# A norm's broadcast, the normalizing of its tiles and the pooled branch, reordered in a two-block transformer kernel

## The chip, the cores and the metric

The kernel runs on one core of one Trainium2 chip. The metric is the device time of one execution in microseconds (us); lower is better. The engines are named as in the profile: PE does the matmuls and the transposes, DVE, ACT and POOL do elementwise work, SP starts the weight loads. Each engine has a queue of its own, and semaphores tie the queues together.

## What is computed

Two stacks of two layers each work on 256 tokens of width 1024; the first stack carries 256 context tokens beside them. Only the first stack's modulated norm, its mixer and the pooled branch in it matter here:

```python
def rms_norm(x, g):
    y = x * lax.rsqrt(jnp.mean(x * x, axis=-1, keepdims=True) + RMS_EPS)
    return y * g

def mod_norm(x, m, i, g):
    return rms_norm(x, g) * (1 + m[:, 3 * i + 1, None]) + m[:, 3 * i, None]

# first stack, layer l: ffn 0, then the mixer, then ffn 1
x = ffn_sublayer(x, m, 0, norm_g[l, 0], ffn_w_in[l, 0], ffn_w_out[l, 0])
h = mod_norm(x, m, 1, norm_g[l, 1])
u = h @ w_in[l]
y = jnp.concatenate([
    gated_conv_mixer(u[..., :OFF_B], u[..., OFF_B:OFF_C], u[..., OFF_C:OFF_P], conv_w[l]),
    multiscale_pool_mixer(u[..., OFF_P:OFF_Q], pool_w[l], pool_scale[l]),   # window mean - itself, @ pool_w
    neighbourhood_attention(q, k, v, kc, vc, rpb[l]),
], axis=-1) @ w_out[l]
x = x + m[:, 5, None] * y
x = ffn_sublayer(x, m, 2, norm_g[l, 2], ffn_w_in[l, 1], ffn_w_out[l, 1])
```

The context goes through the same mixer in layer 0, so that 512 columns are worked on there; in layer 1 its keys and values alone are needed, and the pooled branch has 256 columns. The second stack (`hybrid_layer`) has plain norms, three attentions, and a feed-forward part with a short convolution.

## The kernel before

**Layout.** Activations lie transposed: eight K tiles `X[kt]` of 128 channels by 512 (or 256) tokens. Each large product is made in three matmuls (`mm3`, L129 at `mm`): both operands are split into a rounded high part and the rest (`hi`, `lo`), and hi·hi, hi·lo and lo·hi are added up in PSUM. Weights are split as well (`begin`, L102 on ACT gives `whi`, L103 on DVE gives `wlo`), one chunk ahead of their use.

**Norm.** `modnorm` gives two kinds of operands. `pre` is the tile scaled but not yet normalized (`xhi`, `xlo`); the first projections run on it, and their results are multiplied by the norm's factor afterwards. `ops` are the normalized tiles (`hhi`, `hlo`) that all later projections take, made by `normed()` once the factor is there. `stats` begins the factor: squares, sums over channels on PE (`ms`, L176, into `pt`), the factor `r` (DVE L181, then a power on POOL, L182), and then `over`: four transposes on PE (L189, two for 256 tokens) that spread `r` over the partitions and a copy on DVE into `rb` (L191). A list of steps with ticks sets where in the code these two stand: `tick()` is called at half and at the end of each group of products; both steps have tick 0.

**Normalizing before.** For each K tile: `n = x * rb` on DVE (L238, 512 wide); scale and shift for each half of 256 (ACT L244, or DVE L242 for the second half of odd tiles); `hhi` as ACT's copy of `n` (L102); `hlo = n - hhi` on DVE (L103).

**Mixer (`mix1`).** The w_in chunks are used in the order 4 to 9 (queries, keys, values), 3 (pooled input `u`), then attention for four pairs of heads (scores `sc` L580, softmax on DVE and ACT, transposes `pt` L601, output `o` L678), then chunks 2, 0, 1 (the convolution), then w_out. ACT copies chunk 3's result into `z` (L658); POOL makes the window means from it (`pool_sums`, L730 to L743, then L649 and L650) into `su0` and `su1`. POOL also loads and turns a bias tile `tb` (L565, L566) for each head. At the end of the mixer `su` goes through one matmul each (L715), and w_out takes its eight K tiles in the order 0 to 7: 0 and 1 are the convolution, 2 and 3 the pooled branch, 4 to 7 the attention (`mhi`, `mlo`).

**Order.** The framework's scheduler takes the code as a list and sets the order in which each engine's instructions stand in its queue, by estimates of its own; an instruction can be put ahead of others that were written earlier if it finds room. On the chip each queue runs in the order in which it was laid down. Names below: mix(0), mix(1) are the mixers of layers 0 and 1, ffn(l,s) the feed-forward parts; "filler" are products of a later chunk that the scheduler put between steps of attention.

Of the kernel before, what the change touches and what calls it, by code (L numbers as in the profile page):

```python
# [8 lines left out]
F32 = mybir.dt.float32  # L9
BF16 = mybir.dt.bfloat16  # L10
F32R = mybir.dt.float32r
# [23 lines left out]
class Slots:  # L35
    """Tiles in slots of their own, handed out in the order in which the trace gives them back."""
# [19 lines left out]
class Kernel:  # L56
# [48 lines left out]
    def weights(self, *key):  # L105
        """The split of the next chunk in the order of use; the one after it is begun as well."""
        assert self.order[self.used] == key, (key, self.order[self.used])
        while len(self.ready) < 2 and self.begun < len(self.order):
            self.ready.append(self.begin(*self.order[self.begun]))
            self.begun += 1  # L110
        self.used += 1
        return self.ready.pop(0)
# [14 lines left out]
    def mm(self, *a, **k):  # L127
        """A product; while the chain is on, one after the other as they are written."""
        i = self.nc.tensor.matmul(*a, **k)  # L129
        if self.chain:  # L130
            if self.chained is not None:
                self.after(i, self.chained)
            self.chained = i
# [11 lines left out]
    def project(self, w, width, cols, ops, n):  # L145
        banks = [self.bank("mm") for _ in cols]
        k = len(ops)
        for i in range(k):
            for ps, c in zip(banks, cols):
                self.mm3(ps[:, :n], self.w_at(w, i, width, c), ops[i], i == 0, i == k - 1)  # L150
            if i in (k // 2 - 1, k - 1):
                self.tick()
        return banks
# [40 lines left out]
    def stats(self, X, n, at=(0, 0)):  # L194
        """Begins a norm's statistics; they are finished between the products of the next projections."""
        acc = self.squares(X, n)

        def ms():
            ps = self.bank("pt")
            self.sums(ps, acc, n)  # L200
            self.r = self.rsqrt(ps, n // 128)

        def over():
            self.rb = self.spread(self.r, n // 128)

        self.later(at, ms, over)

    def later(self, at, *steps):
        """Has the steps taken between the products that follow, by their halves."""
        self.steps, self.ticks = list(zip(at, steps)), -1  # L210
        self.tick()
# [6 lines left out]
    def modnorm(self, l, i, n, nd):  # L218
# [13 lines left out]
        self.stats(self.X, n, (0, 0))  # L232
        ops = []

        def normed():
            for kt in range(KT):
                t = self.act(name="n")
                nc.vector.tensor_tensor(t[:, :n], self.X[kt][:, :n], self.rb[:, :n], op=ALU.mult)  # L238
                for r in segs:
                    c = slice(r * 256, r * 256 + 256)  # L240
                    if r and kt % 2:
                        nc.vector.tensor_scalar(t[:, c], t[:, c], self.mod(l, i + 1, kt, r), self.mod(l, i, kt, r), op0=ALU.mult, op1=ALU.add)  # L242
                    else:
                        nc.scalar.activation(t[:, c], t[:, c], AF.Identity, bias=self.mod(l, i, kt, r), scale=self.mod(l, i + 1, kt, r))  # L244
                hi, lo = self.act(F32R, "hhi"), self.act(F32R, "hlo")
                self.split(hi[:, :n], lo[:, :n], t[:, :n])
                self.slots.free(t)
                ops.append((hi, lo))
# [3 lines left out]
    def first_gates(self, finish):  # L252
        """The first norm and two chunks of its gates, begun on the scales alone: the shifts are loaded last."""
# [287 lines left out]
    def preload(self, name):  # L541
        """Has ACT's next table set loaded behind the last function of the one before it."""
# [26 lines left out]
    def attn1(self, q, k, tbs):  # L569
        """The transposed weights of a pair of heads, whose scores take the two halves of the rows."""  # L570
# [34 lines left out]
    def mix1(self, l, fill=()):  # L605
# [80 lines left out]
        self.preload("silu_and_others")  # L686
        C = []
# [24 lines left out]
        for m in range(2):  # L712
            su = SU[m]
            pw = self.bank("mm")
            nc.tensor.matmul(pw[:, :n1], self.poolw[:, l, m, :], su[:, :n1], start=True, stop=True)  # L715
            sc = self.par["pool_scale"][:, l * 2 + m:l * 2 + m + 1]
            mix[2 + m] = hi, lo = pair()
            nc.scalar.activation(hi[:, :n1], pw[:, :n1], AF.Copy, scale=sc)
            nc.vector.scalar_tensor_tensor(out=lo[:, :n1], in0=pw[:, :n1], scalar=sc, in1=hi[:, :n1].bitcast(F32), op0=ALU.mult, op1=ALU.subtract)
        self.slots.free(*SU)  # L720

        for c in range(4):
            w = self.weights("w_out", l, c)
            for m2, ps in enumerate(self.project(w, 256, (0, 128), [(a[:, :n1], b[:, :n1]) for a, b in mix], n1)):
                self.residual(2 * c + m2, ps, l, 5, n1)
# [20 lines left out]
    def pair2(self, one, first, second):  # L746
        """The transposed weights of a pair of heads, whose scores take the two halves of the rows."""
# [83 lines left out]
    def edge(self):  # L831
# [17 lines left out]
        def ms():  # L849
            # r * (r * r * scaled + EPS) ** -0.5 with r = (plain + EPS) ** -0.5  # L850
# [22 lines left out]
    def layer2(self, L):  # L873
# [133 lines left out]
        self.stats(X, 256, (0, 0))  # L1007
# [231 lines left out]
```

## Time and profile before

| | us |
|---|---|
| median of three runs (lowest to highest) | 2641.17 (2639.41 to 2641.89) |
| span of the profiled execution | 2640.9 |
| PE busy | 2588.1 |
| DVE, ACT, POOL busy | 1754.1, 1175.7, 121.6 |

The stages, by the times at which they begin in the trace: ffn(0,0) 0, mix(0) about 409, ffn(0,1) 627, ffn(1,0) 995, mix(1) 1367, ffn(1,1) 1517, the second stack 1709 to the end. The page gives busy time for each engine, the clock granted to PE in tenths of full speed, and the chain of work that ended last. A timeline row is: start, duration, engine, line, operation, tiles, shapes, count; in brackets the idle time of the engine just before it and the instruction that ended it. A row with x4 is four instructions in a row, and its duration is that of all four.

### The profile page before, as it was taken

How to read it: one execution, taken by the hardware profiler on the slowest of the kernel's cores; microseconds unless marked ns; L12 is line 12 of the kernel's file. 1: busy time of each engine (PE TensorE's matmuls, PEld its weight loads, DVE VectorE, ACT ScalarE, POOL GpSimd, SP SyncE). 2: the span in 40 equal slices, each digit the busy share in tenths (PEclk: the TensorE clock that was granted, in tenths of full speed). 3: DMA queues.
4: the chain of work that ended last, by engine and by line, in shares of the span. 5: the costliest groups of instructions: out<-in, count | busy, mean ns of one | idle time of the engine just before them, and what ended most of it. 6: DMA issues, size and time to landing. Idle time of an engine off the chain costs nothing.

```text
span 2640.9 us, 40212 instructions
## 1 busy us (share of the span) xinstructions
PE 2588.1 (98%) x16220; PEld 2251.3 (85%) x16220; DVE 1754.1 (66%) x3259; ACT 1175.7 (45%) x2125; POOL 121.6 (5%) x196
## 2 busy tenths in 40 slices
PE   7999999999999999999999999999999999999999
PEld 5888888668888888888887899987999998799998
DVE  6877755557867758765354665666589866557984
ACT  4322234445222234212344554456556655654664
POOL 1000002200000000000002000002000000200000
PEclk9999999999999999999999999999999999999999
DMA  7545533112545533453233254632454463245444
GB/s 270 207 167 191 181 121 123 54 51 107 189 170 179 177 119 141 176 179 141 72 130 108 96 189 174 207 115 94 161 191 176 166 204 126 96 160 182 173 169 148
DMA packets 61114, 401.70 MB, mean 152 GB/s; under 512 B 7040, under 2 KB 7168, under 8 KB 21632
## 3 DMA queue, kind: packets, MB, share of 16 engines
q1 hardware_dynamic: 59616, 395.20, 42.3%
q0 software_dynamic: 1024, 3.15, 0.4%
q8 instruction: 127, 2.08, 0.3%
q10 hardware_dynamic: 288, 0.79, 0.1%
q14 instruction: 59, 0.48, 0.1%
HBM read 398.06 MB, written 1.05 MB: 151 GB/s over the span
## 4 chain that ended last, share of the span: by engine, by line
PE 85%; issue 8%; DVE 2%; ACT 2%; POOL 1%; DMA 0%; SPq 0%; POOLq 0%; DVEq 0%; ACTq 0%
PE mm L129 78%; PE sc L580 1%; PE sc L752 1%; PE o L804 1%; PE o L678 1%; PE pt L601 1%; DVE wlo L103 1%; PE pt L770 1%; ACT whi L102 1%; POOL ptw L797 1%; POOL nl L787 0%; POOL r L182 0%; PE o L806 0%; DMA raw<-in_w_mod 0%; PE sc L129 0%
## 5 line engine op out<-in xcount | busy, mean ns | idle before, releaser
L102 ACT ACTIVATE whi<-raw 128x1024 fp32r<-128x1024 f32 (+2 forms) x704 | 621.0, 925 | 544.9 <-PE mm L129 272.3
L103 DVE TENSOR_TENSOR wlo<-raw,whi 128x1024 fp32r<-128x1024 f32 (+2 forms) x704 | 730.0, 1065 | 172.4 <-ACT whi L102 171.2
L129 PE MATMUL mm<-hlo,whi 128*128 128x512 f32 (+1 forms) x1520 | 555.7, 366 | 2.9 <-DVE hlo L103 2.9
L129 PE MATMUL mm<-hhi,wlo 128*128 128x512 f32 (+1 forms) x1520 | 555.8, 366 | 0.0
L129 PE MATMUL mm<-hhi,whi 128*128 128x512 f32 (+1 forms) x1520 | 554.4, 366 | 0.0
L129 PEld LDWEIGHTS mm<-hlo,whi 128*128 128x128 f32 x1520 | 286.1, 188 | 54.8 <-DVE hlo L103 3.5
L129 PEld LDWEIGHTS mm<-hhi,wlo 128*128 128x128 f32 x1520 | 285.9, 188 | 52.2 <-issue 2.2
L129 PEld LDWEIGHTS mm<-hhi,whi 128*128 128x128 f32 x1520 | 285.7, 188 | 52.0 <-issue 1.9
L129 PE MATMUL mm<-xg,whi 128*128 128x256 f32 x1600 | 298.3, 286 | 0.0
L485 ACT ACTIVATE t<-mm 128x512 f32<-128x512 f32 (+1 forms) x82 | 44.7, 546 | 520.4 <-PE mm L129 520.4
L129 PEld LDWEIGHTS mm<-xg,whi 128*128 128x128 f32 x1600 | 249.3, 190 | 7.5 <-issue 6.4
L129 PE MATMUL mm<-h,whi 128*128 128x256 f32 x1280 | 227.7, 281 | 0.3
L129 PE MATMUL mm<-xg,wlo 128*128 128x256 f32 x800 | 227.8, 285 | 0.0
L129 PE MATMUL mm<-glo,whi 128*128 128x512 f32 x528 | 208.6, 395 | 0.0
L129 PE MATMUL mm<-ghi,whi 128*128 128x512 f32 x528 | 208.3, 395 | 0.0
L129 PE MATMUL mm<-ghi,wlo 128*128 128x512 f32 x528 | 207.7, 393 | 0.0
L129 PEld LDWEIGHTS mm<-h,whi 128*128 128x128 f32 x1280 | 196.3, 188 | 1.1 <-DVE h L103 1.1
L410 DVE CUSTOM_DVE_ANT_0 junk<-raw,cb,par 128x1024 bf16<-128x1024 f32 x128 | 163.9, 1280 | 49.3 <-DMA raw<-in_w_mod 48.4
L392 DVE SCALAR_TENSOR_TENSOR x<-mm,m,x 128x256 f32<-128x256 f32 x128 | 56.0, 479 | 192.3 <-PE mm L129 191.5
L129 PE MATMUL mm<-h,wlo 128*128 128x256 f32 x640 | 179.1, 281 | 0.0
L410 DVE CUSTOM_DVE_ANT_0 raw<-raw,cb,par 128x1024 f32<-128x1024 f32 x128 | 164.3, 1284 | 3.7
L129 PEld LDWEIGHTS mm<-xg,wlo 128*128 128x128 f32 x800 | 152.4, 190 | 4.1 <-issue 3.6
(270 smaller groups left out, 4099.4 us busy)
## 6 DMA issues: line engine op xcount, KB each, us to landing
raw<-in_ffn_w_in SPq DMA_DIRECT2D x87, 1024.0 KB, 4.8
raw<-in_w_in SPq DMA_DIRECT2D x74, 1024.0 KB, 4.8
raw<-in_w_mod SPq DMA_DIRECT2D x72, 1024.0 KB, 4.8
raw<-in_ffn_w_out SPq DMA_DIRECT2D x64, 704.0 KB, 4.0
raw<-in_w_up SPq DMA_DIRECT2D x44, 1024.0 KB, 4.8
raw<-in_w_down SPq DMA_DIRECT2D x32, 704.0 KB, 4.2
raw<-in_w_out SPq DMA_DIRECT2D x16, 1024.0 KB, 4.8
raw<-in_w_branch SPq DMA_DIRECT2D x12, 1024.0 KB, 4.8
```

What stands on the lines that cost most here:

```text
L102: self.nc.scalar.activation(hi, src, AF.Copy)
L103: self.nc.vector.tensor_sub(lo, src, hi.bitcast(F32))
L129: i = self.nc.tensor.matmul(*a, **k)
L392: self.nc.vector.scalar_tensor_tensor(out=self.X[m][:, c], in0=ps[:, c], scalar=self.mod(l, i, m, r), in1=self.X[m][:, c], op0=ALU.mult, o ...
L410: nc.vector.tensor_tensor_reduce(out=w if r else self.junk, in0=w, in1=self.cb[:, r, :], scale=1.0, scalar=self.par["b_mod"][:, c:c + 1], ...
L485: self.tabled(nc.scalar.activation(g[:, :n], pa[:, :n], AF.Silu))
L580: nc.tensor.matmul(sc[:, :nk], q[r, c0 + qt * 128:c0 + qt * 128 + 128], k[r, c0:c0 + nk], start=True, stop=True)
L601: nc.tensor.transpose(pp[:, kt * 128:kt * 128 + 128], s[:, kt * 128:kt * 128 + 128], self.ident)
L678: nc.tensor.matmul(o[64 * a:64 * a + 64, :256], v[:, h * 64:h * 64 + 64], pts[a][:, kt, :], start=(kt == 0), stop=(kt == len(vs) - 1), til ...
L752: self.nc.tensor.matmul(sc[:, o:o + n], a[r, ca:ca + 128], b[r, cb:cb + n], start=True, stop=True)
L770: nc.tensor.transpose(pp[:, (qt + i) * 128 if qt == 0 or i == 0 else 256:((qt + i) * 128 if qt == 0 or i == 0 else 256) + 128], s[:, a + i ...
L797: nc.gpsimd.tensor_tensor(pt[:, c:c + 128], pt[:, c:c + 128], self.past, op=ALU.mult)
```

## The change

Three edits.

1. `stats` still takes the sums at tick 0; the broadcast step `over` is put at tick 2, and at tick 3 for mix(0) (`i == 3 and n == nd`). A group of pre-products has 24 matmuls and one tick at its end. The second stack's feed-forward norm goes from (0, 0) to (0, 2) as well.
2. `normed()` works on halves of 256 in three steps: DVE makes `n = x * scale * rb`, ACT writes `hhi = n + shift` rounded, DVE makes `hlo = (n + shift) - hhi`.
3. The pooled branch's matmul, `mhi` and `mlo` are written right behind attention, ahead of w_in chunk 2, and w_out takes its K tiles in the order 4, 5, 6, 7, 2, 3, 0, 1.

```diff
-        self.stats(self.X, n, (0, 0))
+        self.stats(self.X, n, (0, 3 if i == 3 and n == nd else 2))
...
             for kt in range(KT):
                 t = self.act(name="n")
-                nc.vector.tensor_tensor(t[:, :n], self.X[kt][:, :n], self.rb[:, :n], op=ALU.mult)
+                hi, lo = self.act(F32R, "hhi"), self.act(F32R, "hlo")
                 for r in segs:
                     c = slice(r * 256, r * 256 + 256)
-                    if r and kt % 2:
-                        nc.vector.tensor_scalar(t[:, c], t[:, c], self.mod(l, i + 1, kt, r), self.mod(l, i, kt, r), op0=ALU.mult, op1=ALU.add)
-                    else:
-                        nc.scalar.activation(t[:, c], t[:, c], AF.Identity, bias=self.mod(l, i, kt, r), scale=self.mod(l, i + 1, kt, r))
-                hi, lo = self.act(F32R, "hhi"), self.act(F32R, "hlo")
-                self.split(hi[:, :n], lo[:, :n], t[:, :n])
+                    sh = self.mod(l, i, kt, r)
+                    nc.vector.scalar_tensor_tensor(out=t[:, c], in0=self.X[kt][:, c], scalar=self.mod(l, i + 1, kt, r), in1=self.rb[:, c], op0=ALU.mult, op1=ALU.mult)
+                    nc.scalar.activation(hi[:, c], t[:, c], AF.Identity, bias=sh)
+                    nc.vector.scalar_tensor_tensor(out=lo[:, c], in0=t[:, c], scalar=sh, in1=hi[:, c].bitcast(F32), op0=ALU.add, op1=ALU.subtract)
...
         self.preload("silu_and_others")
+        for m in range(2):
+            su = SU[m]
+            pw = self.bank("mm")
+            nc.tensor.matmul(pw[:, :n1], self.poolw[:, l, m, :], su[:, :n1], start=True, stop=True)
+            sc = self.par["pool_scale"][:, l * 2 + m:l * 2 + m + 1]
+            mix[2 + m] = hi, lo = pair()
+            nc.scalar.activation(hi[:, :n1], pw[:, :n1], AF.Copy, scale=sc)
+            nc.vector.scalar_tensor_tensor(out=lo[:, :n1], in0=pw[:, :n1], scalar=sc, in1=hi[:, :n1].bitcast(F32), op0=ALU.mult, op1=ALU.subtract)
+        self.slots.free(*SU)
         C = []
         for ps in self.project(self.weights("w_in", l, 2), 256, (0, 128), sl(n1), n1):
...
-            for m2, ps in enumerate(self.project(w, 256, (0, 128), [(a[:, :n1], b[:, :n1]) for a, b in mix], n1)):
+            for m2, ps in enumerate(self.project(w, 256, (0, 128), [(a[:, :n1], b[:, :n1]) for a, b in mix], n1, (4, 5, 6, 7, 2, 3, 0, 1))):
...
         pre = self.xg(g)
-        self.stats(X, 256, (0, 0))
+        self.stats(X, 256, (0, 2))
```

The removed lines of the pooled branch are the added ones, 30 lines further down, behind chunk 1; `project` takes the K order as `turns`. Queues before and after are shown at two places.

**PE at the start of attention in mix(0).** `sc` are scores, `mm<-hhi,whi` fillers (products of chunk 2), `pt` transposes of softmax weights, `su` the pooled branch's operand (`k1_672` is its weight). Before:

```order
L580 MATMUL sc_3671<-k_3297,q_3095 128x512
L580 MATMUL sc_3672<-k_3297,q_3095 128x512
L129 MATMUL mm_4263<-hhi_3117,whi_3595 128x512 [waits Activation_49]
L129 MATMUL mm_4263<-hlo_3118,whi_3595 128x512
L129 MATMUL mm_4263<-hhi_3117,wlo_3596 128x512 [waits DVE_49]
L129 MATMUL mm_4264<-hhi_3117,whi_3595 128x512
L129 MATMUL mm_4264<-hlo_3118,whi_3595 128x512
L129 MATMUL mm_4264<-hhi_3117,wlo_3596 128x512
L129 MATMUL mm_4263<-hhi_3125,whi_3595 128x512
L129 MATMUL mm_4263<-hlo_3126,whi_3595 128x512
L580 MATMUL sc_3703<-k_3297,q_3095 128x512 [waits DVE_49,PE_49]
L580 MATMUL sc_3704<-k_3297,q_3095 128x512 [waits DVE_49,PE_49]
```

After:

```order
L579 MATMUL sc_3679<-k_3305,q_3095 128x512
L579 MATMUL sc_3680<-k_3305,q_3095 128x512
L689 MATMUL mm_4263<-su_3663,k1_672 128x512 [waits DMAHW3_49,Activation_49,Pool_49]
L579 MATMUL sc_3711<-k_3305,q_3095 128x512 [waits DVE_49,PE_49]
L579 MATMUL sc_3712<-k_3305,q_3095 128x512 [waits DVE_49,PE_49]
L600 MATMUL pt_3691<-ident_83,s_3683 128x128 [waits DVE_49]
L600 MATMUL pt_3691<-ident_83,s_3683 128x128 x3
L600 MATMUL pt_3705<-ident_83,s_3697 128x128 [waits DVE_49]
L600 MATMUL pt_3705<-ident_83,s_3697 128x128 x3
L689 MATMUL mm_4269<-su_3668,k1_672 128x512 [waits Activation_49,Pool_49]
L579 MATMUL sc_3756<-k_3305,q_3095 128x256 [waits DVE_49,PE_49]
L579 MATMUL sc_3757<-k_3305,q_3095 128x256 [waits DVE_49,PE_49]
```

Both `su` matmuls now stand behind the first scores, and the scores and transposes of the next steps stand behind them; eight fillers that stood between the two pairs of scores are further back. In mix(1) the two `su` matmuls stand in the same way: two scores, `su_10534`, one score, `su_10539`, and then seven fillers.

**PE at the broadcast of ffn(1,0).** `mm<-xhi` and `mm<-xlo` are pre-products, the `pt<-ones` rows are the sums, `sc<-ident,r` the broadcast's transposes. Before:

```order
L176 MATMUL pt_7391<-ones_84,t_7368 128x1 [waits DVE_49]
L176 MATMUL pt_7391<-ones_84,t_7368 128x1 x3
L129 MATMUL mm_7420<-xhi_7288,wlo_7244 128x258
L129 MATMUL mm_7420<-xhi_7298,whi_7243 128x258
L129 MATMUL mm_7420<-xlo_7299,whi_7243 128x258
L129 MATMUL mm_7420<-xhi_7298,wlo_7244 128x258
L129 MATMUL mm_7420<-xhi_7308,whi_7243 128x258
L129 MATMUL mm_7420<-xlo_7309,whi_7243 128x258
L189 MATMUL sc_7399<-ident_83,r_7396 128x128 [waits Pool_49]
L189 MATMUL sc_7399<-ident_83,r_7396 128x128 x3
```

After:

```order
L177 MATMUL pt_7407<-ones_84,t_7384 128x1 [waits DVE_49]
L177 MATMUL pt_7407<-ones_84,t_7384 128x1 x3
L129 MATMUL mm_7429<-xhi_7304,wlo_7260 128x258
L129 MATMUL mm_7429<-xhi_7314,whi_7259 128x258
...
L129 MATMUL mm_7429<-xhi_7374,whi_7259 128x258
L129 MATMUL mm_7429<-xlo_7375,whi_7259 128x258
L129 MATMUL mm_7429<-xhi_7374,wlo_7260 128x258
L190 MATMUL sc_7479<-ident_83,r_7412 128x128 [waits Pool_49]
L190 MATMUL sc_7479<-ident_83,r_7412 128x128 x3
L129 MATMUL mm_7428<-xhi_7304,whi_7259 128x258 [waits PE_49]
```

The transposes stand 16 matmuls further back, at the end of the second group of 24. At the other norms they stand further back by 40 in mix(0), 2 in ffn(0,1), 19 in mix(1), 17 in ffn(1,1), and 14 and 17 in the second stack's two feed-forward parts.

## Rows read from the trace of the kernel before

**Rows 1.** The page, part 4: the chain that ended last, by engine

```profile
PE 85%; issue 8%; DVE 2%; ACT 2%; POOL 1%; DMA 0%; SPq 0%; POOLq 0%; DVEq 0%; ACTq 0%
```

**Rows 2.** Waits of PE, by releaser: us in total, times, longest

```profile
PE sc L189 <- POOL r L182: 5.1, 8, 0.9
...
PE mm L129 <- DVE hlo L103: 2.9, 1, 2.9
...
PE mm L129 <- DVE mlo L103: 1.4, 2, 0.8
...
PE mm L129 <- ACT mhi L102: 0.5, 1, 0.5
```

**Rows 3.** PE, timeline, start of attention in mix(0), then in mix(1)

```profile
487.37 1.13 PE L580 MATMUL sc<-k,q 64*128 64x512 f32 x4
...
1435.79 1.13 PE L580 MATMUL sc<-k,q 64*128 64x512 f32 x4
```

**Rows 4.** POOL, timeline, pooled sums in mix(0), then in mix(1)

```profile
488.62 1.49 POOL L736 COPY su<-zs 64x512 f32<-64x512 f32 x1
...
495.83 1.28 POOL L650 TENSOR_TENSOR su<-su,z 128x512 f32<-128x512 f32 x1
...
498.20 0.75 POOL L743 COPY su<-zs 64x512 f32<-64x512 f32 x1
...
501.79 1.27 POOL L650 TENSOR_TENSOR su<-su,z 128x512 f32<-128x512 f32 x1
...
1439.58 1.82 POOL L650 TENSOR_TENSOR su<-su,z 128x256 f32<-128x256 f32 x1
...
1445.80 0.79 POOL L650 TENSOR_TENSOR su<-su,z 128x256 f32<-128x256 f32 x1
```

**Rows 5.** Stretches: us; busy PE, PEld, DVE, ACT, POOL; PE clock; DMA

```profile
487.30:503.00 15.70, 14.28 (x69) 8.48 (x68) 13.05 (x34) 9.49 (x23) 15.10 (x14) 1.00 0.20 67
503.00:518.00 15.00, 14.90 (x73) 7.49 (x72) 11.36 (x43) 10.22 (x30) 3.14 (x7) 1.00 0.09 28
995.00:1002.00 7.00, 6.11 (x37) 5.70 (x37) 4.23 (x9) 2.06 (x5) 1.39 (x1) 0.76 0.40 140
1367.00:1374.00 7.00, 6.11 (x38) 5.75 (x37) 4.85 (x10) 1.35 (x3) 1.38 (x1) 0.76 0.43 149
1435.80:1447.00 11.20, 10.16 (x47) 5.57 (x47) 9.20 (x32) 7.31 (x15) 10.11 (x17) 1.00 0.46 178
```

**Rows 6.** PE, timeline, the broadcasts of mix(0) and mix(1)

```profile
412.05 0.65 PE L189 MATMUL sc<-ident,r 128*128 128x128 f32 x4 [0.90 <-POOL r L182]
...
1370.36 1.08 PE L189 MATMUL sc<-ident,r 128*128 128x128 f32 x4 [0.89 <-POOL r L182]
```

**Rows 7.** Timeline around mix(1)'s wait for a normalized tile: PE, DVE, POOL

```profile
1385.99 0.85 PE L129 MATMUL mm<-hhi,whi 128*128 128x512 f32 x3
1389.71 0.50 PE L129 MATMUL mm<-hlo,whi 128*128 128x512 f32 x1 [2.87 <-DVE hlo L103]
1390.05 0.39 PE L129 MATMUL mm<-hhi,wlo 128*128 128x512 f32 x1
...
1383.70 2.94 DVE L238 TENSOR_TENSOR n<-x,rb 128x512 f32<-128x512 f32 x2
...
1383.62 4.88 POOL L566 TENSOR_TENSOR tb<-k,tb 128x384 f32<-128x384 f32 x4 [0.93 <-DMA tb<-in_rpb]
```

**Rows 8.** Groups of DVE, 412 to 424.5 us (mix(0)): busy us, mean ns of one

```profile
L238 DVE TENSOR_TENSOR n<-x,rb 128x512 f32<-128x512 f32 x8 | 5.1, 682 | 0.0
L103 DVE TENSOR_TENSOR hlo<-n,hhi 128x512 fp32r<-128x512 f32 x6 | 3.9, 683 | 0.0
...
L242 DVE TENSOR_SCALAR n<-n,m,m 128x256 f32<-128x256 f32 x3 | 1.2, 407 | 0.0
```

**Rows 9.** DVE, timeline: two steps of 256 with two tensors and a scalar

```profile
407.61 0.89 DVE L229 SCALAR_TENSOR_TENSOR xlo<-x,m,xhi 128x256 fp32r<-128x256 f32 x2
```

**Rows 10.** Stretch with mix(0)'s normalized tiles, columns as in rows 5

```profile
412.70:431.00 18.30, 18.30 (x112) 16.31 (x111) 17.94 (x31) 14.25 (x27) 10.56 (x10) 1.00 0.33 105
```

More of the change, by code (lines that the diff above doesn't have):

```diff
@@ L143, in w_at, with project @@
         return w[0][:, c:c + n], w[1][:, c:c + n]
-    def project(self, w, width, cols, ops, n):
+    def project(self, w, width, cols, ops, n, turns=None):
         banks = [self.bank("mm") for _ in cols]
         k = len(ops)
-        for i in range(k):
+        turns = turns or range(k)
+        for j, i in enumerate(turns):
             for ps, c in zip(banks, cols):
-                self.mm3(ps[:, :n], self.w_at(w, i, width, c), ops[i], i == 0, i == k - 1)
-            if i in (k // 2 - 1, k - 1):
+                self.mm3(ps[:, :n], self.w_at(w, i, width, c), ops[i], j == 0, j == k - 1)
+            if j in (k // 2 - 1, k - 1):
                 self.tick()
@@ L711, in mix1 @@
             self.split(mix[m][0][:, :n1], mix[m][1][:, :n1], Y[m][:, :n1])
[L712 to L720, printed above, removed]
         for c in range(4):
             w = self.weights("w_out", l, c)
-            for m2, ps in enumerate(self.project(w, 256, (0, 128), [(a[:, :n1], b[:, :n1]) for a, b in mix], n1)):
+            for m2, ps in enumerate(self.project(w, 256, (0, 128), [(a[:, :n1], b[:, :n1]) for a, b in mix], n1, (4, 5, 6, 7, 2, 3, 0, 1))):
                 self.residual(2 * c + m2, ps, l, 5, n1)
```

## The prediction

> **What bounds the kernel now.** I read the chain of waits first, then PE's waits by releaser, then the places of the three edits in the timelines. The chain is PE for 85% of the span and "issue" for 8% [rows 1]: the time changes where PE stands still, or where its granted clock falls. The waits that the change is about are short. PE waits for the broadcast's factor 5.1 us in eight places, once for a normalized tile, 2.9 us, and at the two ends of the mixers 1.4 + 0.5 us for the last operands of w_out [rows 2]. The broadcast wait can also cost clock. In mix(0) the four transposes behind a wait of 0.90 took 0.65 us; in mix(1), behind 0.89, they took 1.08 [rows 6], and from 1367 to 1374 the mean granted clock is 0.76 [rows 5], that is a part of the stretch at 1.2 instead of 2.4 GHz: 7 x 0.24 = 1.7 us. ffn(1,0) has the same, 0.76 from 995 to 1002 [rows 5]; mix(0) has 1.00 behind its wait [rows 10].
>
> Attention in the mixers has no room on PE. From 487.3 to 503, the first pair of heads in mix(0), PE is idle for 15.70 - 14.28 = 1.42 us, from 503 to 518 for 0.10, and from 1435.8 to 1447, the start in mix(1), for 1.04 [rows 5]. POOL, elsewhere idle, is busy for 15.10 of the 15.70 us: it makes the pooled sums [rows 5].
>
> **The pooled branch (edit 3).** The queues decide here. Before, the two `su` matmuls stood at the mixer's end, long after the sums; behind the first scores stood eight fillers, whose operands were there, and more fillers between the later steps. After, the first `su` matmul stands right behind the first two scores of mix(0), the second four transposes later; in mix(1) two scores and one score stand ahead of them. Whatever stands behind them on PE waits too: the next scores, so their softmax on DVE and ACT, so the first outputs.
>
> In mix(0) PE gets to `su0` at about 487.37 + 1.13 = 488.5 [rows 3]. POOL finishes `su0` at 495.83 + 1.28 = 497.1 and `su1` at 501.79 + 1.27 = 503.1 [rows 4]. POOL's early steps were stretched by other work: the copy L736 took 1.49 us at 488.6, the like copy L743 0.75 at 498.2 [rows 4]. Taking such stretching off I estimate at best 495.1 and 500.6. The first stall is then 6.6 to 8.6 us. Behind it come the `su` matmul, two scores and eight transposes, some 3.1 us, so the second stall is 2.4 to 2.9. Together 9.0 to 11.5, less the 1.42 that PE idled there anyway: 7.6 to 10.1. I take the lower end, 7.5: DVE has little to do while PE stands.
>
> In mix(1) PE is there at 1435.79 + 1.13 = 1436.9 [rows 3]. `su0` is done at 1439.58 + 1.82 = 1441.4 and `su1` at 1445.80 + 0.79 = 1446.6 [rows 4]; with the last two steps of `su0` at the pace of `su1` (0.79 instead of 1.82), and less elsewhere, 1439.3 and 1443.9. Stalls of 2.4 to 4.5, then some 1.0 us of work, then 3.6 to 4.2: 6.0 to 8.7, less 1.04: 5.0 to 7.7. I take 5.5. The fillers put off are not lost, but they must run later, and PE has 0.10 us in 15 to take them in [rows 5]; so both stalls count in full. Each is longer than the wait that brought the clock down at 1370, so a stretch at half clock may follow each of the four. Behind a first stall it mostly lies ahead of the second, where PE waits anyway; 0 to 5 us, and I take one stretch, 1.7.
>
> In return the ends of the mixers lose their waits: 1.4 + 0.5 = 1.9 us [rows 2]. With K tiles 4 to 7 first, 24 matmuls for two banks lie ahead of the late operands, so all of it is hidden: -1.9 (bounds -1.9 and 0).
>
> A row shows that PE's queue does not let ready matmuls pass. At 1389.71 `hlo,whi` had waited 2.87 us, and `hhi,wlo` ran only behind it at 1390.05, although the hi·hi products had run at 1385.99, so that `hhi` was there [rows 7]. The Trainium skill says the same in PSUM — Partial Sum Buffer, Engine vs sequencer instructions: weight loads may be taken ahead, but "MATMULs start and complete in program order". By that, and the trace agrees, the stalls are paid in full.
>
> **The broadcast and the tiles (edits 1 and 2).** DVE's work for a tile does not get shorter. Before, 8 x 0.682 + 8 x 0.683 and four L242 of 0.407 are 12.5 us for eight tiles [rows 8]. After, there are 32 steps of 256 with two tensors and a scalar; two such took 0.89 together [rows 9], so 12.8 to 14.2 us. ACT loses work, but ACT is not who is waited for. So the tiles come later by as much as `rb` comes later, and PE must find other work meanwhile. By place:
>
> - mix(0): transposes 40 matmuls further back. At about 0.12 us each that is 4.8 us, less the wait of 0.90 and some: `rb` comes 3.4 us later. From 412.7 to 431 PE had no gap, and DVE was busy for 17.94 of 18.30 us [rows 10], so DVE has nothing to catch up with. Gone: 0.9. New, at the tiles: 0 to 4.9 (3.4 and 1.5 of longer work), I take 3.4: net +2.5 (bounds -0.9 and 4.0).
> - ffn(0,1): two matmuls further back, 0.24 us, so most of the wait stays, and DVE's longer work may show: +0.5 (bounds -0.2 and 2).
> - ffn(1,0): 16 matmuls, 1.9 us, cover the 0.89 and, if PE does not stand, the 1.7 of half clock. `rb` is 1 us later: some 0.6 comes back at the tiles. -2.0 (bounds -2.6 and 0.5).
> - mix(1): 19 matmuls cover the same 0.89 + 1.7. But the tiles' end does not follow: while POOL turned four `tb` tiles (4.88 us from 1383.62) DVE's steps took 1.47 instead of 0.68 each, and that led to the wait of 2.87 [rows 7, 8]. With 12.8 us and more of DVE work and the same `tb`, the last tile comes about when it came, so what PE gains ahead it waits for there: -0.5 (bounds -5.4, all three gone, and 2).
> - ffn(1,1) and the second stack's two: the rest of the 5.1, some 1.5 us, covered by 14 to 17 matmuls: -1.5 (bounds -1.5 and 0).
>
> That `tb` row is where a rule bears on edit 2: the Trainium skill, GPSIMD Engine Reference, Key points, says that POOL shares its SBUF interfaces with DVE and contends with DVE instructions that have two SBUF inputs. The new steps have two as well, so by it the slowing stays; the rows here agree (1.47 beside 0.68), and no row shows the new form beside POOL.
>
> **The sum.** Against the profiled execution of 2640.9 us (its median of three is 2641.17, so I add 0.3 at the end): +7.5 + 5.5 + 1.7 - 1.9 + 2.5 + 0.5 - 2.0 - 0.5 - 1.5 = +11.8. That gives 2652.7, with the 0.3 about 2653. With the stalls and the clock at their bounds and the other terms where they are it is 2651 to 2661.
>
> **The rivals.**
> Faster: PE works past the waiting `su` matmuls, or their operands are ready in time. Then the 13 us and the 1.7 are gone, and by the same token waits at the tiles shrink: -0.9 - 0.2 - 2.6 - 4 - 1.5 - 1.9 = -11 at best, 2630. It decides if `su0` of mix(0) is there within 3 us of the first scores instead of 6.6. For it: the removed waits are real. Against it: the order of the queue, the row at 1390.05, and POOL busy 15.10 of 15.70 us. Chance 0.12.
> No change: POOL runs at its fast pace while PE and DVE stand, the clock does not fall, and the tiles of mix(0) and mix(1) are covered (-0.9 and -5.4): 7.5 + 5.0 - 1.9 - 0.9 + 0.5 - 2.0 - 5.4 - 1.5 = +1.3, 2642. For it: L743's 0.75 beside 1.49. Against it: DVE is full in mix(0). Chance 0.18.
> Much slower: POOL's sums end no earlier than in the trace, the clock falls behind every stall and the tiles of mix(0) come late: 10.1 + 7.7 + 5 + 4.0 + 0.5 - 5.9 = +21.4, 2663. For it: a wait of 0.9 was enough to bring the clock down at two places. Chance 0.12.
> The forecast holds the rest, 0.58.
>
> **How the numbers follow.** A measurement of this kernel can tell about 0.2%, 5.3 us. Faster by more than that holds the first rival, 0.12; within it the second, 0.18; slower the forecast and the last, 0.70. Predicted 2653. The range leaves out the first rival and the far end of the last: 2637 to 2664.
>
> **What the new profile would show.** If right: PE idle for 6 us and more before an L689 matmul near 488 and for 2 to 3 us before the second, in mix(1) two waits of 2 to 5 us near 1437, all released by POOL L649; the first `o` of mix(0) comes about 5 us later behind the first scores; no wait before L190 in ffn(1,0), mix(1) and later; no wait for `mhi` or `mlo` at the first w_out products. In mix(0) PE waits for `hlo`. The prediction is wrong if L689 starts without a wait, if POOL's sums take half the time that they took, or if the half-clock stretches go without new ones.

## The result

The changed kernel takes 2663.51 us, the kernel before 2641.18: ratio 1.0085, 95% interval 1.0072 to 1.0098. The profiled execution's span is 2662.5 us against 2640.9. The forecast had the sign and, at 2653, half of the size.

The sums for a norm (PE, L176 before, L177 after) stand at the start of each stage, and the first scores split the mixers. Start to start, in us:

| stage | before | after | moved |
|---|---|---|---|
| mix(0), up to the first scores | 78.1 | 83.0 | +4.9 |
| mix(0), first scores to the end | 139.6 | 148.4 | +8.8 |
| ffn(0,1) | 368.6 | 368.9 | +0.3 |
| ffn(1,0) | 372.0 | 369.1 | -2.9 |
| mix(1), up to the first scores | 68.2 | 63.3 | -4.9 |
| mix(1), first scores to the end | 80.9 | 97.0 | +16.0 |
| ffn(1,1) and the two later feed-forward parts | 572.2 | 573.4 | +1.2 |
| the second stack's two attentions | 545.0 | 543.0 | -2.0 |

The last row is not the change's: the attentions there have stretches at half clock in both kernels, and took between 269.5 and 274.0 us each in the kernels below without any edit to them. The waits of PE in the changed kernel (us in total, times, longest), beside [rows 2]:

```profile
PE mm L689 <- POOL su L649: 14.8, 3, 8.6
...
PE mm L129 <- DVE hlo L245: 3.1, 5, 1.1
...
PE mm L129 <- ACT hhi L244: 2.3, 5, 0.6
...
PE mm L129 <- ACT h L102: 1.4, 2, 0.8
...
PE mm L129 <- DVE h L103: 0.8, 2, 0.4
...
PE sc L190 <- POOL r L183: 0.7, 2, 0.6
```

The broadcast's 5.1 us are down to 0.7, the waits for `mhi` and `mlo` are gone, the single wait of 2.9 for a tile is gone. In their place stand the `su` matmuls with 14.8, and 7.6 in small waits for normalized tiles (`hlo`, `hhi`, `h`). PE at the start of attention in mix(0) and then in mix(1), beside [rows 3]:

```profile
492.37 1.13 PE L579 MATMUL sc<-k,q 64*128 64x512 f32 x4
502.12 2.08 PE L689 MATMUL mm<-su,k 128*128 128x512 f32 x2 [8.63 <-POOL su L649]
504.13 2.08 PE L579 MATMUL sc<-k,q 64*128 64x512 f32 x4
506.14 1.17 PE L600 MATMUL pt<-ident,s 128*128 128x128 f32 x8
507.86 1.13 PE L689 MATMUL mm<-su,k 128*128 128x512 f32 x2 [0.55 <-DVE nmx L594]
...
1442.10 1.13 PE L579 MATMUL sc<-k,q 64*128 64x512 f32 x4
1447.74 1.22 PE L689 MATMUL mm<-su,k 128*128 128x256 f32 x2 [4.52 <-POOL su L649]
1448.90 2.07 PE L579 MATMUL sc<-k,q 64*128 64x512 f32 x2
1452.67 1.22 PE L689 MATMUL mm<-su,k 128*128 128x256 f32 x2 [1.70 <-POOL su L649]
1453.33 0.77 PE L129 MATMUL mm<-hhi,whi 128*128 128x256 f32 x1
...
1454.96 0.41 PE L129 MATMUL mm<-hhi,whi 128*128 128x256 f32 x1
1455.31 2.07 PE L579 MATMUL sc<-k,q 64*128 64x512 f32 x2
1457.31 1.11 PE L600 MATMUL pt<-ident,s 128*128 128x128 f32 x4
...
1470.55 3.67 PE L677 MATMUL o<-ptw,v 128*64 128x256 f32 x14
1474.15 1.12 PE L600 MATMUL pt<-ident,s 128*128 128x128 f32 x4
```

The same scores and transposes in mix(1) before:

```profile
1441.86 1.12 PE L580 MATMUL sc<-k,q 64*128 64x512 f32 x2
1442.92 0.66 PE L601 MATMUL pt<-ident,s 128*128 128x128 f32 x4
```

PE stands for 8.6 us in front of one matmul, with scores behind it in the queue. (For the 0.55 the profile names DVE's `nmx`; POOL's `su1` was done at 507.81, 0.05 us ahead of the matmul, and the two are counted together here.) The durations tell the rest. In mix(1) two scores took 2.07 us and four transposes 1.11 behind the stall, against 1.12 and 0.66 before; in mix(0) eight transposes took 1.17 at 506.14, so the clock was back there after about 4 us of work. The granted clock of mix(1)'s attention (columns as in [rows 5]; the last three are clock, DMA share, GB/s), first after, then before:

```profile
1448.00:1453.00 5.00, 3.30 (x5) 1.08 (x6) 1.63 (x6) 1.72 (x5) 4.47 (x12) 0.50 0.59 210
1453.00:1458.00 5.00, 5.00 (x14) 3.09 (x14) 1.22 (x7) 0.81 (x2) 0.49 (x1) 0.50 0.16 39
1463.00:1470.00 7.00, 7.00 (x15) 2.71 (x14) 3.10 (x13) 2.60 (x6) 0.00 (x0) 0.50 0.00 0
1470.00:1480.00 10.00, 9.74 (x39) 4.69 (x38) 6.07 (x24) 4.67 (x12) 0.00 (x0) 0.71 0.00 1
```

```profile
1447.00:1460.00 13.00, 12.78 (x62) 5.82 (x63) 10.64 (x44) 9.25 (x23) 2.95 (x4) 1.00 0.11 32
1460.00:1476.00 16.00, 15.93 (x100) 9.85 (x96) 7.10 (x29) 10.13 (x22) 0.00 (x0) 1.00 0.00 0
```

Before, the same attention runs at 2.4 GHz throughout. After, it runs at 1.2 GHz from the first stall to about 1475, some 30 us, with PE busy all the time from 1453 on (5.00 of 5.00, 7.00 of 7.00). Seven products of chunk 2 ran in it right behind the second stall, at 1453.33 to 1455.4; the clock came back behind fourteen outputs `o`, and the next product ran at 1493.3 only. Busy time hides it: the page gives PE 98% in both kernels.

### The profile page after: what moved, and what is told of

The parts are those of the page before. It is cut to its first block, busy times and chain, and to the rows that moved or that the text cites. A ratio compares the mean times of both kernels' runs of the same rounds, so it can differ in the third digit from the quotient of the medians.

```text
span 2662.5 us, 40212 instructions
## 1 busy us (share of the span) xinstructions
PE 2598.0 (98%) x16220; PEld 2248.3 (84%) x16220; DVE 1760.5 (66%) x3307; ACT 1158.9 (44%) x2101; POOL 126.9 (5%) x196
```

## The experiments

Each kernel was timed against the kernel before on the same chip; the median there was 2639.5 to 2641.8. Stage times come from one profiled execution of each kernel. Behind the first scores, kernels with the same K order of w_out and no stall there agree within 0.5 us, but for one that is named below. Ahead of attention they scatter more: with the same code and the same order of every queue, mix(0) took 83.0 us in the changed kernel and 81.5 in the one with the first `su` matmul alone early, and mix(1) took 63.1 to 66.1.

**The pooled branch back at the mixer's end**, the rest as changed.

```diff
         self.preload("silu_and_others")
-        for m in range(2):
-            ...                                # su matmul, mhi, mlo
         C = []
...
+        for m in range(2):
+            ...
         for c in range(4):
             w = self.weights("w_out", l, c)
```

> The changed kernel with the pooled branch's matmul, mhi and mlo put back behind chunk 1, at the end of the mixer; the broadcast, the three-step tiles and the K order of w_out stay. Theory (the stalls at the su matmuls and the half clock behind them are the loss): the changed kernel loses 8.8 us between the first scores and the next norm's sums in mix(0) and 16.0 us in mix(1); both go, and 0.5 to 1.5 us of the waits at the mixer's end may come back. About 2663.5 - 24.8 + 1 = 2640, that is 2636 to 2641. Rival (the tiles that come later are the loss, and PE would have waited elsewhere without the su matmuls): the loss stays for the most part, 2655 or more.

2638.42 us, ratio 0.9988 (0.9978 to 0.9997). mix(0) behind the first scores is 138.8 us, mix(1) 79.1, both below the kernel before. That is the K order of w_out, 0.8 and 1.9 us: edits 1 and 2 alone, further down, leave the two at 139.6 and at 80.9 and 81.0. So the pooled branch's place costs 148.4 - 138.8 = 9.6 us in mix(0) and 97.0 - 79.1 = 17.9 in mix(1). The rival is out.

**Edit 3 alone, on the kernel before.**

```diff
+        for m in range(2):
+            ...                                # ahead of chunk 2, as in the change
...
-            for m2, ps in enumerate(self.project(..., n1)):
+            for m2, ps in enumerate(self.project(..., n1, (4, 5, 6, 7, 2, 3, 0, 1))):
```

> The kernel before with edit 3 alone: pooled branch ahead of chunk 2, K order 4 to 7 first. Theory: the su matmuls stand right behind the first scores as in the changed kernel, so the same 8.8 and 16.0 us are lost: 2641.2 + 24.8 = 2666, 2660 to 2668. Rival: without the later tiles there is little to wait for, 2640 to 2648.

2664.66 us, ratio 1.0088 (1.0073 to 1.0103); 148.9 us and 96.6 us behind the first scores. The loss is there without the other two edits.

**The pooled branch one step later**, behind chunk 2.

```diff
-        for m in range(2):                     # pooled branch
-            ...
         C = []
         for ps in self.project(self.weights("w_in", l, 2), 256, (0, 128), sl(n1), n1):
             ...
+        for m in range(2):
+            ...
         Y = []
```

> The changed kernel with the pooled branch written one step later, behind chunk 2 instead of ahead of it, K order kept; chunk 2's products are the fillers then and the su matmuls stand behind them. Theory: the sums are long done when PE comes to the su matmuls, no stall, no half clock in attention, and the mixer's end has no wait either: 2635 to 2640. Rival: as with the branch at the end, 2655 or more.

2638.74 us, ratio 0.9995 (0.9984 to 1.0006); 138.8 and 79.3 us. The `su` matmuls stand behind chunk 2's products in the queue then. As I read these orders, the scheduler fills with what is next in the code and ready by its estimates; in the change that was the pooled branch, whose operand POOL had not made yet.

**Early in mix(1) only**, at the end in mix(0).

```diff
-        for m in range(2):
-            ...
+        if l == 1:
+            ...                                # both, early
...
+        if l == 0:
+            ...                                # both, behind chunk 1
```

> The changed kernel with the pooled branch at the end in mix(0) and early in mix(1) only. Theory: the two mixers' losses are apart from each other, so mix(1) keeps its 16.0 us, of which the two stalls are 6.2 and the rest is clock: PE's granted clock is 0.50 for about 30 us of its attention, and the time is that of the kernel with both at the end plus 14 to 17. Rival (the clock falls in mix(1) because of what happened in mix(0) or by chance): the clock in mix(1)'s attention is back within 4 us, and the time is that of the kernel with both at the end plus 5 to 8.

2654.67 us, ratio 1.0057 (1.0042 to 1.0072), 16.3 above the kernel with both at the end; 97.3 us behind the first scores of mix(1), and clock 0.50 from about 1434 to 1465. Mix(1) loses this by itself.

**Only the first `su` matmul early, in mix(1).**

```diff
+        if l == 1:
+            pooled(0)                          # early; pooled(1) and mix(0)'s stay at the end
```

> The changed kernel with the pooled branch at the end, but for the first of the two su matmuls in mix(1), which stands right behind the first scores as in the changed kernel: one stall of 4.5 us instead of 4.5 and 1.7. Theory (one stall brings the clock down, and the attention's steps do not bring it back): granted clock 0.50 for 25 to 30 us and 2638.4 + 3.5 + 10 = 2652, 2649 to 2654. Rival (it takes both stalls): half clock for a few us at most, 2641 to 2645.

2651.67 us, ratio 1.0036 (1.0023 to 1.0050), with a wide spread: ten times from 2641.3 to 2654.5. In the profiled execution there is one stall of 4.5 us, and the clock behind it is as low as with two:

```profile
1435.00:1440.00 5.00, 4.37 (x12) 2.95 (x12) 0.86 (x4) 0.81 (x2) 4.63 (x10) 0.50 0.53 210
1440.00:1450.00 10.00, 10.00 (x24) 5.13 (x24) 4.12 (x17) 2.71 (x6) 3.86 (x7) 0.50 0.13 39
1450.00:1460.00 10.00, 10.00 (x26) 3.80 (x26) 4.97 (x23) 4.63 (x11) 0.00 (x0) 0.50 0.00 0
1460.00:1470.00 10.00, 9.63 (x48) 4.47 (x44) 6.35 (x26) 5.41 (x14) 0.00 (x0) 0.91 0.01 2
```

One stall is enough in this execution, and eighteen products of chunk 2 among the scores behind it, at 1436.3 to 1443.0, did not bring the clock back; it rose at about 1461.8, again behind fourteen outputs `o`. The spread of the times goes with the clock: the four runs of 2641.3 to 2646.9 us have a mean granted clock of 0.995 to 0.997, the six of 2651.5 to 2654.5 one of 0.990 to 0.992. So by the clock the long stretch came in six runs of ten, in one and the same kernel. What tells them apart is not shown.

**The same two stalls, with dense products behind them.** In mix(1) chunk 2's products stand among the first two pairs of heads. The pooled sums are also written earlier there, both ahead of the first pair.

```diff
         for p in range(4):
...
-            if p in (1, 2):
+            if p in (1, 2) and not last:
                 sums(p - 1)
+            if last and p < 1:
+                sums(0)
+                sums(1)
+            if last and p == 1:
+                pooled(0)
+                pooled(1)
+                chunk2()                       # project(w_in 2), from behind attention
```

> The changed kernel with the pooled branch at the end in mix(0); in mix(1) it is early, as in the changed kernel, and chunk 2's products, which there come behind attention, are put behind the second su matmul, among the steps of the first two pairs of heads. The two waits for the sums stay. Theory (the clock that fell in the stall stays at half because attention's own steps do not bring it back, and dense products do): the granted clock is 1.00 again within 10 us of the second su matmul instead of 25, and the time is 2654.7 less 7 to 10 us: 2644 to 2648. Rival (the clock stays at half for a time of its own after such a stall, whatever runs): half clock for 25 us and more, 2652 to 2657.

2645.71 us, ratio 1.0024 (1.0014 to 1.0033). The waits in front of the two `su` matmuls are 3.43 and 1.97 us, not quite the 4.52 and 1.70 of the changed kernel, and then:

```profile
1442.00:1446.00 4.00, 3.07 (x4) 1.00 (x4) 0.77 (x4) 1.17 (x3) 0.94 (x4) 0.50 0.00 0
1446.00:1450.00 4.00, 4.00 (x25) 3.92 (x25) 3.52 (x11) 1.90 (x4) 0.00 (x0) 0.68 0.00 0
1450.00:1460.00 10.00, 10.00 (x73) 7.60 (x71) 1.78 (x5) 4.14 (x7) 0.00 (x0) 1.00 0.32 107
```

```profile
1442.93 1.22 PE L667 MATMUL mm<-su,k 128*128 128x256 f32 x2 [1.97 <-POOL su L649]
...
1446.85 0.56 PE L129 MATMUL mm<-hhi,whi 128*128 128x256 f32 x1
...
1448.28 0.41 PE L129 MATMUL mm<-hhi,whi 128*128 128x256 f32 x1
1448.49 0.64 PE L600 MATMUL pt<-ident,s 128*128 128x128 f32 x4
```

The clock is back within 6 us of the second stall. mix(1) behind the first scores is 87.8 us: 8.7 above the kernel without stalls, 9.5 below the one with the stalls and without the products. So of the 17.9 us of mix(1) about half goes when the clock is back after some 10 us instead of 30, and the rival, a stretch of fixed length, is out. That the dense products are what brought it back is not shown. When it rose, seven of them had run behind scores and transposes; in the changed kernel seven ran as well, right behind the second stall, and eighteen in the kernel with one `su` matmul early, and there it stayed down. The pooled sums and the first stall differ here too.

**Edit 1 alone** and **edit 2 alone**, each on the kernel before.

```diff
-        self.stats(self.X, n, (0, 0))
+        self.stats(self.X, n, (0, 3 if i == 3 and n == nd else 2))
```

> The kernel before with edit 1 alone: broadcast at tick 2, 3 in mix(0), and tick 2 in the second stack's feed-forward parts. Theory (what the tiles lose in mix(0) is the late broadcast): the part of mix(0) ahead of attention is 3 to 5 us longer than before (78.1), ffn(1,0) 2 to 3 us shorter than its 372.0, the part of mix(1) ahead of attention 1 to 3 shorter than its 68.2: 2638 to 2642 in all. Rival (it is the three-step tiles): mix(0) unchanged, 2634 to 2637.

```diff
-                nc.vector.tensor_tensor(t[:, :n], self.X[kt][:, :n], self.rb[:, :n], op=ALU.mult)
+                    nc.vector.scalar_tensor_tensor(out=t[:, c], ...)     # normed() as changed
```

> The kernel before with edit 2 alone: tiles of 256 in three steps. Theory (the late broadcast is the loss in mix(0)): mix(0) ahead of attention stays within 1 us of 78.1; in mix(1) the tiles gain 1 to 3 us: 2638 to 2641. Rival (three steps are longer on DVE): mix(0) 3 to 5 us longer, 2643 to 2647.

Edit 1: 2642.80 us, ratio 1.0011 (1.0002 to 1.0021), 0.8 above what I expected. Edit 2: 2639.49, ratio 1.0004 (0.9993 to 1.0015). By stage, in us:

| | before | edit 1 | edit 2 | both, pooled branch at the end |
|---|---|---|---|---|
| mix(0) up to the first scores | 78.1 | 81.5 | 83.3 | 83.0 |
| ffn(1,0) | 372.0 | 370.0 | 370.5 | 369.6 |
| mix(1) up to the first scores | 68.2 | 65.3 | 63.2 | 63.1 |
| second stack's feed-forward parts | 380.0 | 381.4 | 380.0 | 381.4 |

My expectation that mix(0) would stand still with edit 2 alone was wrong: it loses 5.2 us there with `rb` as early as before. Edit 1 alone loses 3.4, with one wait of 2.2 us for ACT's `hhi` and a stretch at half clock; the two do not add up, since together they lose 4.9. DVE's groups in mix(0) from 412 to 440 (busy us, mean ns), of before and then of edit 2 alone:

```profile
L103 DVE TENSOR_TENSOR hlo<-n,hhi 128x512 fp32r<-128x512 f32 x8 | 6.9, 889 | 0.0
...
L238 DVE TENSOR_TENSOR n<-x,rb 128x512 f32<-128x512 f32 x8 | 5.1, 682 | 0.0
L242 DVE TENSOR_SCALAR n<-n,m,m 128x256 f32<-128x256 f32 x4 | 2.3, 583 | 0.0
```

```profile
L245 DVE SCALAR_TENSOR_TENSOR hlo<-n,m,hhi 128x256 fp32r<-128x256 f32 x16 | 10.5, 712 | 0.0
L243 DVE SCALAR_TENSOR_TENSOR n<-x,m,rb 128x256 f32<-128x256 f32 x16 | 7.6, 525 | 0.0
```

14.3 us became 18.1. In that kernel PE waits 1.9 us for the last `hlo` of mix(0), and a stretch at half clock follows.

**mix(0)'s broadcast alone back at tick 0**, pooled branch at the end.

```diff
-        self.stats(self.X, n, (0, 3 if i == 3 and n == nd else 2))
+        self.stats(self.X, n, (0, 0 if i == 3 and n == nd else 2))
```

> The changed kernel with the pooled branch at the end and with the broadcast of mix(0) alone back at tick 0. Theory (late broadcast): mix(0) ahead of attention is 78 to 79 instead of 83.0, so 2638.4 - 4.5 = 2634, 2632 to 2636. Rival (three-step tiles): 82 to 83 as with tick 3, 2637 to 2640.

2638.30 us, ratio 0.9994 (0.9985 to 1.0003); mix(0) up to the first scores 81.8. The time is the rival's, and the tiles are late without the late broadcast. A share for the broadcast is not shown: the 1.3 us to the 83.0 are no more than the scatter of this stage (81.5 with tick 3 and the same queues).

**Without POOL's work on the bias tiles**, pooled branch at the end. It leaves out the subtraction of the bias from the mask, which the attention needs.

```diff
         self.after(nc.gpsimd.dma_start(tb, self.t["rpb"][l, h]), self.power)
-        nc.gpsimd.tensor_tensor(tb, self.colmask[:, None, :].to_broadcast([128, 6, 64]), tb, op=ALU.subtract)
```

> The changed kernel with the pooled branch at the end, without POOL's subtraction on the bias tiles (the mask is left out of the attention's bias; the loads stay). Theory (the three-step tiles are late in mix(0) because each step takes longer while POOL works on the bias tiles, 18.1 us of DVE for the sixteen halves' steps instead of 14): those steps take 0.40 to 0.48 each throughout, the wait for hlo in mix(0) goes, mix(0) ahead of attention is 78 to 80 instead of 83.0, 2638.4 - 4 = 2634, 2632 to 2636. Rival (the steps are too many in any case): 82 to 83, 2637 to 2639.

2632.92 us, ratio 0.9977 (0.9968 to 0.9986); mix(0) up to the first scores 78.7, mix(1) 61.8. (Behind mix(0)'s first scores it is 141.6, with a stretch at half clock there that was not followed up.) DVE's steps in mix(0):

```profile
L245 DVE SCALAR_TENSOR_TENSOR hlo<-n,m,hhi 128x256 fp32r<-128x256 f32 x16 | 6.8, 491 | 0.0
L243 DVE SCALAR_TENSOR_TENSOR n<-x,m,rb 128x256 f32<-128x256 f32 x16 | 6.8, 489 | 0.0
```

13.6 us instead of 18.0 in the same kernel with POOL's work, where `hlo` took 0.76 us a step and `n` 0.48; the broadcast is at tick 3 in both, and the queues of PE, DVE and ACT have the same order. So the three-step tiles are late in mix(0) because POOL works on the bias tiles at the same time.

**What gained, together.**

```diff
-        self.stats(self.X, n, (0, 3 if i == 3 and n == nd else 2))
+        self.stats(self.X, n, (0, 2 if l == 1 and n == 512 else 0))
...
-        return pre, ops, normed
+        return pre, ops, normed4 if i == 3 and n == nd else normed      # normed4: the four steps of before, in mix(0)
...
-        self.stats(X, 256, (0, 2))
+        self.stats(X, 256, (0, 0))
```

and the pooled branch at the mixer's end, K order as changed.

> What gained in the runs so far, together: three-step tiles everywhere but in mix(0), which keeps the four steps of before; broadcast at tick 2 in ffn(1,0) and mix(1) only, at tick 0 elsewhere; pooled branch at the mixer's end; K order of w_out 4, 5, 6, 7, 2, 3, 0, 1. Theory (the parts add up by stage): mix(0) ahead of attention 78.1 as before, mix(0) behind the first scores 138.8 instead of 139.6, ffn(1,0) 369.6 instead of 372.0, mix(1) 142 to 145 instead of 149.1, the second stack's feed-forward parts as before: 7 to 10 us less than the kernel before, 2631 to 2634. Rival (what is gained ahead is waited for behind): 2637 to 2641.

2632.19 us, ratio 0.9971 (0.9962 to 0.9981), 0.3% below the kernel before: its highest time, 2634.3, lies under the lowest of that kernel on the same chip, 2635.4. The stages are as expected: mix(0) 78.1 and 138.8, ffn(1,0) 369.6, mix(1) 143.7, the second stack's feed-forward parts 380.0.

## Why the prediction was right in sign and half in size

| term | forecast | measured |
|---|---|---|
| stalls at `su`, mix(0), net of the idle time of before | +7.5 | 8.63 + 0.55 - 1.42 = +7.8 |
| stalls at `su`, mix(1), net | +5.5 | 4.52 + 1.70 - 1.04 = +5.2 |
| half clock behind them | +1.7 (0 to 5) | (9.6 - 7.8) + (17.9 - 5.2) = +14.5 |
| ends of the mixers | -1.9 | -0.8 - 1.9 = -2.7 |
| mix(0), tiles and broadcast | +2.5 (-0.9 to 4.0) | +4.9 |
| ffn(0,1) | +0.5 | +0.3 |
| ffn(1,0) | -2.0 | -2.9 |
| mix(1), tiles and broadcast | -0.5 (-5.4 to 2) | -4.9 |
| ffn(1,1), second stack | -1.5 (-1.5 to 0) | +1.2 |

**The stalls** were right in place, order and total: the order of PE's queue and POOL's times of before gave their sums to within 0.3 us net, and the first `o` of mix(0) came 20.6 us behind the first scores instead of 13.2. That the sums came out so closely is in part luck, since I had taken lower ends for a reason that was wrong: POOL would run faster while DVE stands. It did not; its steps in mix(0) after, beside [rows 4]:

```profile
493.61 1.48 POOL L734 COPY su<-zs 64x512 f32<-64x512 f32 x1
...
500.81 1.26 POOL L649 TENSOR_TENSOR su<-su,z 128x512 f32<-128x512 f32 x1
...
503.17 0.61 POOL L741 COPY su<-zs 64x512 f32<-64x512 f32 x1
...
506.54 1.27 POOL L649 TENSOR_TENSOR su<-su,z 128x512 f32<-128x512 f32 x1
```

`su0` was done 9.7 us behind the first scores both times, and while DVE was idle, from 499.91 to 506.24, the last step of `su0` took 1.26 us against 1.28 before; only the copy was shorter, 0.61 against 0.75. In both mixers the first stall was at its upper end (8.63 of 6.6 to 8.6, 4.52 of 2.4 to 4.5) and the second short (0.55 instead of 2.4 to 2.9, 1.70 instead of 3.6 to 4.2), because the work between them ran at half clock: there the remark held that the clock behind a first stall is hidden by the second. (Between the two `su` matmuls of mix(0) stand two scores and eight transposes; the "four transposes later" of the prediction is a slip that its sum does not use.)

**The half clock** is the term that failed: 1.7 with an upper bound of 5, measured 14.5, which is what is left of the mixers' losses when the stalls are taken off. In mix(0) my price was right. There PE was busy for 4.2 us at half clock, half of that, 2.1, is lost, and the remainder is 1.8. In mix(1) it was busy for 26.3 us at half clock, 13.1 lost, and the remainder is 12.7. So the step that failed is the length of the drop in mix(1). I priced it at the stretch that the kernel before shows behind its short waits, where pre-products follow and the clock is back within the 7 us windows of [rows 5]; no row told how long it stays down in attention. The length is not fixed: 10 us in mix(0) and with chunk 2's products moved up, some 30 in mix(1) of the change, and in the kernel with one early `su` matmul long in six runs of ten, by their mean clock. The changed kernel's own four runs go the same way: one took 2656.6 us at a mean clock of 0.994, the others 2662.9 to 2664.3 at 0.988 to 0.990. What work brings the clock back stays open. In mix(0) it came back behind `su`, scores and transposes alone, in mix(1) behind outputs, and products ran at half clock in between without raising it.

**The ends of the mixers** gained 2.7 by the K order, more than the 1.9 of waits that I took as the bound. Where the other 0.8 comes from no run shows.

**The tiles in mix(0)** cost more than my upper bound. I counted DVE's new steps at the pace of a row without POOL beside it, [rows 9], and put the whole contention into "the same as before". The 12.5 us of before were too few as well: that window ends at 424.5, with six of the eight `hlo` steps, and over the whole it is 14.3. 32 short steps suffer more from POOL than 20 long ones: 18.1 instead of 14.3 us. The sentence on the Trainium skill's GPSIMD Engine Reference, Key points, that I set beside it (contention with DVE instructions that have two SBUF inputs) pointed the right way, and the kernel without POOL's work agrees (0.49 us a step for both forms, instead of 0.53 and 0.71 with edit 2 alone); the size came from the runs alone.

**mix(1)** gained nearly all that its bounds allowed. The forecast held that its last tile comes when it came before; in the profiled execution it came earlier, since there it was POOL that was held up (next section but one). The size of this gain is partly the draw of that execution: with the code of before the stage took 68.2 and 66.8 us (the kernel before and edit 3 alone), with the changed code 63.1 to 66.2.

**ffn(1,1) and the second stack** went past my bound of zero: +0.7, +0.4 and +0.1 in the three feed-forward parts. The wait for the factor went from 0.5 to nothing in the second stack's first one, but the tiles behind a later `rb` were waited for, 0.7 for ACT's `h` and 0.4 for DVE's. A wait that is removed by coming later is only gained if what hangs on it has slack. Edit 1 alone shows it too, +0.7 in each of the second stack's two.

Of the rivals, "much slower" gave 2663, with 2663.5 measured, and had a chance of 0.12. That is luck in its sum: it counted 17.8 for the stalls and 5 for the clock, falling four times, where 13.0 and 14.5 were measured; the clock fell twice and stayed down once.

## To carry to other kernels

Look at where the scheduler puts a hoisted instruction in an in-order queue, and read from the trace of before when its operand is ready: that alone gave the 13 us of stalls. Price a stall on PE by the clock behind it too, and give that term a wide bound: stalls of a few us cost 1.8 us of clock in mix(0) and 12.7 in mix(1), and a short drop seen elsewhere was no price for it. Look at the granted clock, since busy time hides it. And the time of a step under contention is to be taken from the stretch in which it will run, not from a quiet one.

## What the runs showed of the hardware

The granted clock can stay at 1.2 GHz while PE is busy all the time: from 1440 to 1460 in the kernel with one early `su` matmul, 20.0 of 20.0 us at 0.50. The same instructions run at 1.00 in the kernel before, where no long stall comes ahead of them. And it need not stay down: in four of the ten runs of the kernel with one early `su` matmul the mean clock is 0.995 to 0.997, as high as the kernel before shows on that chip (0.992 to 0.997).

DVE and POOL can slow each other in two ways for the same instructions. In mix(1), with the queues of DVE, ACT and POOL in the same order, three `tb` steps of POOL took 11.43 us in one kernel (pooled branch at the end) and 4.28 in another (mix(0)'s broadcast at tick 0 besides); DVE's steps beside them went the other way. First the one (its second row gives shortest, median and longest of the mixer's `tb` steps in ns: one took 9.1 us), then the other:

```profile
1383.11 11.43 POOL L565 TENSOR_TENSOR tb<-k,tb 128x384 f32<-128x384 f32 x3 [1.95 <-DMA tb<-in_rpb]
...
L565 POOL TENSOR_TENSOR tb<-k,tb x6: 1004/1181/9145, 1383.1 to 1402.8; 128x384 f32<-128x384 f32 x6
```

```profile
L245 DVE SCALAR_TENSOR_TENSOR hlo<-n,m,hhi 128x256 fp32r<-128x256 f32 x16 | 8.3, 574 | 0.0
L243 DVE SCALAR_TENSOR_TENSOR n<-x,m,rb 128x256 f32<-128x256 f32 x16 | 6.8, 480 | 0.0
```

```profile
1381.27 4.28 POOL L565 TENSOR_TENSOR tb<-k,tb 128x384 f32<-128x384 f32 x3 [1.99 <-DMA tb<-in_rpb]
```

```profile
L245 DVE SCALAR_TENSOR_TENSOR hlo<-n,m,hhi 128x256 fp32r<-128x256 f32 x16 | 9.8, 665 | 0.0
...
L243 DVE SCALAR_TENSOR_TENSOR n<-x,m,rb 128x256 f32<-128x256 f32 x16 | 8.2, 571 | 0.0
```

With POOL held up mix(1) took 63.1 us up to the first scores, with DVE slowed 66.1; three more kernels with the same code there took 64.6, 64.7 and 66.2, so there are values between. What decides was not tried.
